# Softmax denominators from a column of ones beside the values, and a separate tile for the last sum of squares

## The chip, the cores and the metric

The kernel runs on one core of one Trainium2 chip. The metric is the device time of one execution in microseconds (us), on the slowest core where there are several; here there is one. Of several runs the median is given.

## The reference

One layer of a decoder: a half-step SwiGLU feed-forward part, a mixer, and a second half-step feed-forward part, each between two RMS norms, on 512 rows of 1024 columns in float32. The mixer runs two branches side by side and joins them with one output matrix: a gated linear recurrence (LRU) over 512 channels, and attention with a sliding window, 8 query heads of 64 columns that share 2 key and value heads, and a learned sink for each head. Cut to what the change touches:

```python
def sliding_window_sink_attention(q, k, v, sinks):      # blocks of 128 queries
    ...
    scores = jnp.einsum("bnqkgd,bnjkd->bnkgqj", qb, k_band).astype(jnp.float32) * scale
    ...
    scores = jnp.where(mask[None, :, None, None], scores, MASK_VALUE)   # window of 128 keys
    sink = sinks.astype(jnp.float32).reshape(1, 1, N_KV_HEADS, GQA_GROUP, 1, 1)
    m = jnp.maximum(jnp.max(scores, axis=-1, keepdims=True), sink)
    p = jnp.exp(scores - m)
    denom = jnp.sum(p, axis=-1, keepdims=True) + jnp.exp(sink - m)
    p = (p / denom).astype(v.dtype)
    out = jnp.einsum("bnkgqj,bnjkd->bnqkgd", p, v_band)
    ...
def reference(x, ...):
    x = x + 0.5 * rms_norm(swiglu(rms_norm(x, ffn1_pre_g), ffn1_w_gu, ffn1_w_down), ffn1_post_g)
    y = hybrid_mixer(rms_norm(x, mix_pre_g), ...)        # LRU and attention, then w_o
    x = x + rms_norm(y, mix_post_g)
    x = x + 0.5 * rms_norm(swiglu(rms_norm(x, ffn2_pre_g), ffn2_w_gu, ffn2_w_down), ffn2_post_g)
    return x
```

## The kernel before

Names: `P` is 128 (partitions, and rows of a block), `T` 512 rows, `NB` 4 blocks of rows, `HD` 64, `D` 1024, `KC` 4 chunks of 128 channels of the LRU. The instructions of each engine run in the order in which the program issues them (the schedule is written out by hand), and an engine that waits holds up all that stands behind in its queue. TensorE (PE) multiplies into the 8 banks of PSUM, which `bank(name)` hands out in turn; large products are made in three passes from a high and a low part of each operand. VectorE is `dve` (DVE), ScalarE `act` (ACT), GpSimd `pool` (POOL), the DMA queue of SyncE `sync`.

**Where the operands of the softmax live.** One wide tile `home` of 2048 columns holds four regions of 512: `k0` (first block's keys), `q0` (first block's queries), `neg` (a mask value for the first block), and `v`, the value rows turned to (key, head and column) by PE at L1512 and copied there. After the first block's scores `k0`, `q0` and `neg` are not read again.

**The softmax.** Its units are pairs (b, n): block b of 128 queries, n one of the two key heads, four query heads in each. A loop over `now` from 0 to 9 runs three stages of different units in a pipeline, and fills PE's queue in between:

- `scores(now)`: PE's products for a block when n is 0 (L1610 in the first block, L1621 after); DVE brings the part of the window that lies in the block before into one tile of 128 x 256 for two heads by a predicated copy (L1637), takes the maximum (L1638), makes the negated row maximum `nm` (L1641) and the sink's exponent `es` (L1643).
- `pump`: the next of PE's other products, those of the LRU's gates `gt`, which DVE scales (L1426).
- `turn_p(now - 1)`: PE transposes the four probability tiles (L1664), ACT copies them out (`pa`, L1666), and GpSimd masks them into the part of the block before, `pp` (L1670), and of the block itself, `pa` (L1671).
- `exps(now)`: ACT's four exponentials (L1652), each with `accum_out`, so that each is followed by a read of ACT's accumulator into `dsum`; the exponential of `es` (L1653); and GpSimd's sum of both (L1656), the denominators of the unit.
- the LRU's steps that are due: ACT's tanh and exponential, GpSimd's square `m` (L1578), DVE's `th` (L1581). At `now` 5, after the values of that step, ACT takes four square roots (L1584); at `now` 6, after the values of that step, which are those of unit (2,0), the products `xc<-xc,th` follow (L1587; two on GpSimd, two on DVE) and two scans (L1592).
- `values(now - 2)`: PE's value products into `po` (L1683, L1684); one bank holds both units of a block. After the second unit DVE takes the reciprocal of eight denominators (L1688) and multiplies 512 columns of `po` by them into `yn` (L1691); ACT squares `yn` for the norm (L1693).

After the loop come the scan of chunk 0 and the low part `wlo` of an output weight (L185, a deferred step of DVE), the root and reciprocal of the norm, the scaling of the four `yn` (L1708 on ACT, L1710 on DVE), their transposes on PE (L1762), and the output matrix.

**The tail.** The last feed-forward part ends with four blocks of rows; the last block is cut into three pieces. For each piece DVE adds the product to the sum `y` (L1983), ACT squares it with a sum into a column of the tile `ss` (L1984), and DVE multiplies it by the gain row (L1988). Then the sums are added (L1986, L1990), ACT takes the root (L1995), DVE the reciprocal (L1996), scales and adds the residual (L1999), and DMAs write the rows (L2000).

Of the kernel before, what the change touches and what calls it, by code (L numbers as in the profile page):

```python
# [8 lines left out]
F32 = mybir.dt.float32  # L9
F32R = mybir.dt.float32r  # L10
U8 = mybir.dt.uint8
AF = mybir.ActivationFunctionType
ALU = mybir.AluOpType
# [108 lines left out]
def tile_layer(ctx: ExitStack, tc: tile.TileContext, out: bass.AP, **ins: bass.AP):  # L122
# [18 lines left out]
    def bank(name):  # L141
        return psum.tile([P, T], F32, tag="bank", name=name)

    def t2k(name, dt=F32):
        return big.tile([P, T], dt, tag="t2k", name=name, bufs=NT2K)
# [16 lines left out]
    def wt(name, w=T, dt=F32):  # L162
        return tmp.tile([P, w], dt, tag="w", name=name, bufs=NW)
# [1155 lines left out]
    def masks():  # L1319

        home.append(wide("home"))
        neg = home[0][:, 2 * T:3 * T]
        upf = wt("upf")
        pool.memset(neg, 1.0)
        pool.affine_select(v4(upf), v4(neg), pattern=[[0, NB], [1, P]], base=0, channel_multiplier=-1, compare_op=ALU.is_gt, fill=0.0)
        pool.memset(neg, MASK_VALUE)
        dve.tensor_copy(up8f, upf)
        return neg
# [149 lines left out]
    mx.spread()  # L1478
    R = mx.R
    xps = [conv_in(ci, b) for ci, b in enumerate(xl_banks)]  # L1480
    k0, q0 = home[0][:, :P], home[0][:, T:2 * T]

    def in_parts(b, first, name, low=dve):

# [18 lines left out]
    for j in range(4):  # L1503
        b = in_product(f"pq{j}")
        if j < KC - 1:
            split_xc(j + 1)
        lru_gates(j)
        qT.append(in_parts(b, q0[:, j * P:(j + 1) * P], f"qT{j}", deferred if j == 3 else dve))
        if j == 0:
            vt = bank("vt")  # L1510
            for b in range(NB):
                pe.transpose(vt[:, b * P:(b + 1) * P], vT[:, b * P:(b + 1) * P], ident)  # L1512
            v = home[0][:, 3 * T:]
            dve.tensor_copy(v, vt)
    preload(AF.Exp)


# [105 lines left out]
    def scores(b, n):  # L1623
        if n == 0:
            products(b)
        mx_ = small.tile([P, 4], F32, tag="mx", name=f"mx{b}{n}")
        if b == 0:
            cur, = score_banks[b, n]
            dve.copy_predicated(cur, up8f, neg)
            dve.tensor_reduce(mx_, v4(cur), op=ALU.max, axis=AX.X)  # L1630
            heads = [cur[:, j * P:(j + 1) * P] for j in range(4)]
        else:
            heads = []
            for i, both in enumerate(score_banks[b, n]):
                both = both.rearrange("p (j w k) -> p j w k", j=2, w=2)
                cur = both[:, :, 1, :]
                dve.copy_predicated(cur, up8[:, :2, :], both[:, :, 0, :])  # L1637
                dve.tensor_reduce(mx_[:, 2 * i:2 * i + 2], cur, op=ALU.max, axis=AX.X)  # L1638
                heads += [both[:, j, 1, :] for j in range(2)]
        nm = small.tile([P, 4], F32, tag="nm", name=f"nm{b}{n}")  # L1640
        dve.scalar_tensor_tensor(nm, mx_, -scale, nsink[:, 4 * n:4 * n + 4], op0=ALU.mult, op1=ALU.min)  # L1641
        es = small.tile([P, 4], F32, tag="es", name=f"es{b}{n}")
        dve.tensor_add(es, nm, sinks[:, 4 * n:4 * n + 4])  # L1643
        unit[b, n] = heads, nm, es

    def exps(b, n):
        heads, nm, es = unit[b, n]
        dsum = small.tile([P, 4], F32, tag="dsum", name=f"dsum{b}{n}")
        sc = wt(f"sc{b}{n}")
        for j in range(4):  # L1650
            hs = slice(j * P, (j + 1) * P)
            act.activation(sc[:, hs], heads[j], AF.Exp, bias=nm[:, j:j + 1], scale=scale, accum_out=dsum[:, j:j + 1])  # L1652
        act.activation(es, es, AF.Exp)  # L1653
        if n == 0:
            unit[b] = small.tile([P, 8], F32, tag="den", name=f"den{b}")
        pool.tensor_add(unit[b][:, 4 * n:4 * n + 4], dsum, es)  # L1656
        unit[b, n] = sc

    def turn_p(b, n):
# [13 lines left out]

    def values(b, n):
        pc, pp = unit[b, n]
        if n == 0:
            unit[b, "o"] = bank(f"po{b}")
        po = unit[b, "o"]
        for j in range(4):
            hs = slice(j * P, (j + 1) * P)  # L1680
            o = po[:, (4 * n + j) * HD:(4 * n + j + 1) * HD]
            if b > 0:
                pe.matmul(o, pp[:, hs], v[:, (b - 1) * P + n * HD:(b - 1) * P + (n + 1) * HD], start=True, stop=False)  # L1683
            pe.matmul(o, pc[:, hs], v[:, b * P + n * HD:b * P + (n + 1) * HD], start=b == 0, stop=True)  # L1684
        if n == 0:
            return
        rden = small.tile([P, 8], F32, tag="rden", name=f"rden{b}")
        dve.reciprocal(rden, unit[b])  # L1688
        yn = t2k(f"yn{b}")
        h8 = lambda t: t.rearrange("p (h d) -> p h d", h=8)  # L1690
        dve.tensor_mul(h8(yn), h8(po), rden.unsqueeze(2).to_broadcast([P, 8, HD]))  # L1691
        yns.append(yn)
        sum_of = lambda: act.activation(wt(f"junk{b}"), yn, AF.Square, accum_out=ssq[:, b:b + 1])  # L1693
        if b < NB - 1:
            later(now, sum_of)
        else:
            sum_of()
# [277 lines left out]
    for tb in range(NB):  # L1975
        end = tb == NB - 1
        last = []
        ss = small.tile([P, 3], F32, tag="ss3", name=f"ss_b{tb}")
        tot = small.tile([P, 1], F32, tag="tot", name=f"tot_b{tb}")
        for i, (dh, c0, c1) in enumerate(pieces[tb]):  # L1980
            out_products(tb, i, range(f0 + 2 * ((tb, i) in started), f1))
            y = parts[tb, dh][:, c0:c1]
            dve.scalar_tensor_tensor(y, place(tb, i), -1.0 if dh else 1.0, y, op0=ALU.mult, op1=ALU.subtract if dh else ALU.add)  # L1983
            act.activation(wt(f"ysq{tb}{i}")[:, :c1 - c0], y, AF.Square, accum_out=ss[:, i:i + 1])  # L1984
            if end and i == 2:
                dve.tensor_add(tot, ss[:, 0:1], ss[:, 1:2])  # L1986
            last.append(wt(f"last{tb}{i}")[:, :c1 - c0])
            (dve if end or i else pool).tensor_mul(last[i], y, grow[dh][:, c0:c1])  # L1988
        if end:
            dve.tensor_add(tot, tot, ss[:, 2:3])  # L1990
        else:
            dve.tensor_add(tot, ss[:, 0:1], ss[:, 1:2])

        rs = small.tile([P, 1], F32, tag="rs1", name=f"rs_b{tb}")
        act.activation(rs, tot, AF.Sqrt, bias=eps4, scale=4.0 / D)  # L1995
        dve.reciprocal(rs, rs)  # L1996
        for i, (dh, c0, c1) in enumerate(pieces[tb]):
            y = parts[tb, dh][:, c0:c1]
            dve.scalar_tensor_tensor(y, last[i], rs, x_rows[tb][:, dh * T + c0:dh * T + c1], op0=ALU.mult, op1=ALU.add)  # L1999
            (act if end and i == 1 else sync).dma_start(out[0, tb * P:(tb + 1) * P, dh * T + c0:dh * T + c1], y)  # L2000
# [28 lines left out]
```

## Time and profile before

| | |
|---|---|
| time, median of 3 runs | 845.67 us (845.57 to 845.91) |
| span of the profiled execution | 843.6 us, 2.1 us below the median of the runs |
| PE busy | 834.5 us, 99% of the span |
| DVE, ACT, POOL busy | 87%, 62%, 24% |
| chain that ended last | PE 97% |
| the softmax, 405 to 462 us of the span | PE busy 56.63 of 57.00 us, DVE 51.88, ACT 47.97, POOL 33.58 |
| after the last product, 836 to 844 us | PE busy 0.67 of 8.00 us, DVE 3.62, ACT 1.60 |

The profiled execution is one run, and times within it are counted from its start. A row of a timeline gives the start and the duration in us, the engine (PEld is PE's load of weights, which overlaps its products), the line, the operation, output tile <- input tiles, the shape, and how many instructions were joined in the row; in brackets stands the idle time of the engine just before and the instruction that ended it. The durations of neighbouring instructions of PE overlap, since its passes are pipelined: the distance between their starts is what each costs. "po L1684" names tile and line.

### The profile page before, as it was taken

The numbers are of one execution on the slowest core, as the hardware profiler recorded it, in microseconds if no ns is written. First come the engines' busy times: TensorE is split into PE (matmuls) and PEld (weight loads), VectorE is DVE, ScalarE is ACT, GpSimd is POOL, SyncE is SP. The second block draws the span as 40 slices with busy tenths as digits, with TensorE's granted clock in tenths as the row PEclk, the third lists the DMA queues.
The fourth block names the chain that finished last, engine by engine and source line by source line (L and its number), as shares of the span: only waits on it lengthen the run. The fifth ranks groups of instructions, "written<-read, shape, count | busy, mean of one in ns | idle before, by whom it ended". The sixth has DMA issues, their size and how long they took to land.

```text
span 843.6 us, 12618 instructions
## 1 busy us (share of the span) xinstructions
PE 834.5 (99%) x4568; PEld 722.6 (86%) x4568; DVE 732.7 (87%) x1020; ACT 523.8 (62%) x874; POOL 201.7 (24%) x214
## 2 busy tenths in 40 slices
PE   9999999999999999999999999999999999999996
PEld 8988888988988998997788899888888888888885
DVE  4978999998979865889899589799998998998996
ACT  6646856666666655456788457436757767666552
POOL 2023000140320333334646055112004113032001
PEclk9999999999999999999999999999999999999999
DMA  7249419397595799222511131169539939769742
GB/s 251 77 131 348 151 59 322 80 254 254 129 248 185 169 261 343 77 79 91 158 50 51 50 110 42 50 137 273 186 108 231 322 91 249 249 154 262 295 137 101
DMA packets 123615, 143.75 MB, mean 170 GB/s; under 512 B 23896, under 2 KB 81568, under 8 KB 123040
## 3 DMA queue, kind: packets, MB, share of 16 engines
q1 hardware_dynamic: 109232, 111.86, 41.6%
q0 software_dynamic: 14176, 30.94, 17.0%
q8 instruction: 36, 0.59, 0.3%
q14 instruction: 27, 0.22, 0.1%
q10 hardware_dynamic: 144, 0.13, 0.0%
HBM read 100.45 MB, written 40.89 MB: 168 GB/s over the span
## 4 chain that ended last, share of the span: by engine, by line
PE 97%; ACT 1%; DVE 1%; DMA 1%; issue 0%; POOL 0%; DVEq 0%; POOLq 0%; ACTq 0%
PE ab L955 10%; PE aa L955 10%; PE da L955 5%; PE db L955 5%; PE yaa L1345 3%; PE bb L955 3%; PE ba L955 3%; PE yda L1345 2%; PE ya L507 2%; PE ya L505 2%; PE ya L506 2%; PE a_first L1205 1%; PE aa L885 1%; PE yab L1875 1%; PE yab L1874 1%; PE yab L1876 1%
## 5 line engine op out<-in xcount | busy, mean ns | idle before, releaser
L1115 POOL DMA_DIRECT2D yp_a<-stage x42 | 36.9, 1085 | 181.2 <-ACT stage L1112 160.9
L1115 POOL DMA_DIRECT2D yp_b<-stage x42 | 36.4, 1091 | 144.6 <-ACT stage L1112 121.1
L505 PE MATMUL ya<-hha,whi_ad 128*128 128x512 f32 x62 | 24.1, 389 | 0.0
L506 PE MATMUL ya<-hla,whi_ad 128*128 128x512 f32 x62 | 24.1, 389 | 0.0
L507 PE MATMUL ya<-hha,wlo_ad 128*128 128x512 f32 x62 | 24.1, 389 | 0.0
L688 POOL TENSOR_TENSOR acca_r<-acca_r,sq_r 128x512 f32<-128x512 f32 x6 | 8.2, 1359 | 51.4 <-ACT sq_r L536 51.4
L1988 POOL TENSOR_TENSOR last<-yp,grow 128x512 f32<-128x512 f32 x3 | 3.9, 1290 | 57.7 <-DVE yp L1983 57.7
L524 PE MATMUL an<-xh_mx,whi_xl 128*128 128x256 f32 x64 | 15.8, 287 | 0.0
L1984 ACT ACTIVATE ysq<-yp 128x512 f32<-128x512 f32 (+1 forms) x9 | 5.3, 585 | 16.5 <-DVE yp L1983 16.0
L525 PE MATMUL an<-xh_mx,wlo_xl 128*128 128x256 f32 x64 | 15.5, 283 | 0.0
L505 PE MATMUL gt<-xh_mx,whi_gt 128*128 128x512 f32 x32 | 14.2, 444 | 0.0
L1112 ACT COPY stage<-yab 128x512 f32<-128x512 f32 x12 | 6.5, 604 | 11.7 <-DMA yp_b<-stage 7.4
L507 PEld LDWEIGHTS ya<-hha,wlo_ad 128*128 128x128 f32 x62 | 11.6, 188 | 2.4
L506 PEld LDWEIGHTS ya<-hla,whi_ad 128*128 128x128 f32 x62 | 11.6, 188 | 2.4
L505 PEld LDWEIGHTS ya<-hha,whi_ad 128*128 128x128 f32 x62 | 11.6, 188 | 2.4
L536 ACT ACTIVATE sq_r<-yp_a 128x256 f32<-128x256 f32 (+1 forms) x10 | 5.0, 502 | 12.9 <-DVE yp_a L678 5.9
L505 PE MATMUL pq<-xh_mx,whi_q 128*128 128x512 f32 x32 | 12.8, 400 | 0.0
L505 PE MATMUL pub<-xh_f,whi_bu 128*128 128x512 f32 x32 | 12.6, 395 | 0.0
L507 PE MATMUL gt<-xh_mx,wlo_gt 128*128 128x512 f32 x32 | 12.6, 394 | 0.0
L505 PE MATMUL pgb<-xh_f,whi_bg 128*128 128x512 f32 x32 | 12.6, 393 | 0.0
L506 PE MATMUL gt<-xl_mx,whi_gt 128*128 128x512 f32 x32 | 12.5, 392 | 0.0
L580 ACT ACTIVATE xh_f<-xT,cols 128x256 fp32r<-128x256 f32 x16 | 8.1, 509 | 7.0 <-DVE xT L719 6.4
(2014 smaller groups left out, 3535.0 us busy)
## 6 DMA issues: line engine op xcount, KB each, us to landing
yp_a<-stage POOLq DMA_DIRECT2D x50, 256.0 KB, 8.9
yp_b<-stage POOLq DMA_DIRECT2D x50, 256.0 KB, 9.2
h_a<-za SPq DMA_DIRECT2D x16, 256.0 KB
hxa<-h_a SPq DMA_DIRECT2D x16, 256.0 KB
h_b<-zb SPq DMA_DIRECT2D x16, 256.0 KB
hxb<-h_b SPq DMA_DIRECT2D x16, 256.0 KB
xn<-in_x SPq DMA_DIRECT2D x8, 256.0 KB
xT_hbm<-xT POOLq DMA_DIRECT2D x2, 1024.0 KB, 9.7
```

The lines of the kernel that those rows point to most:

```text
L505: pe.matmul(ps, hi[:, k, :], xh, start=start, stop=False)
L506: pe.matmul(ps, hi[:, k, :], xl, start=False, stop=False)
L507: pe.matmul(ps, lo[:, k, :], xh, start=False, stop=stop)
L524: pe.matmul(ps[:, sl], hi[:, k, :], xh, start=k == 0, stop=False)
L525: pe.matmul(ps[:, sl], lo[:, k, :], xh, start=False, stop=False)
L885: pe.matmul(o, w[:, k, js], x, start=first and i + j + k == 0, stop=k == 3 and i == 2, skip_group_check=True)
L955: pe.matmul(b[tb], x[:, blk], w[:, k, :], start=first and q + k + j == 0, stop=q + k == 2 and j == 2, skip_group_check=True)
L1115: pool.dma_start(o, st.rearrange("p (a b) -> p a b", a=2) if len(o.shape) == 3 else st, accum_op=ALU.add)
L1205: pe.matmul(banks[j][:, HALF[0]], ws[j][part][:, k, :], n1.xs[k][xpart][:, HALF[0]], start=k == 0 and part == xpart, stop=stop and k == KD ...
L1345: pe.matmul(o, a[:, k, ms], x[:, js], start=first and i + k + m % 2 == 0, stop=k == 1 and i == 2, skip_group_check=True)
L1874: pe.matmul(banks[i], hh[:, js], hi[:, k, :], start=first and k == 0, stop=False, skip_group_check=True)
L1875: pe.matmul(banks[i], hh[:, js], lo[:, k, :], start=False, stop=False, skip_group_check=True)
```

## The change

The wide tile is divided anew: 128 columns of keys, 512 of queries, 512 of the mask value, and then 8 value groups (4 blocks by 2 key heads) of 65 columns, 64 of values and one of ones, which GpSimd sets ahead of the softmax. The value products of a head are 65 columns wide, and the 65th is the sum of the masked probabilities. So the exponentials have no `accum_out`, and `dsum` and GpSimd's sum of the denominators go. `nm` and `es` of a block are tiles of eight columns, and `es` is made once for a block, after its second unit's maximum. Each unit has a bank `po` of its own, 4 x 65 columns, and right after its value products DVE adds `es` to the four sums in PSUM, takes the reciprocal, and multiplies the unit's 256 columns into its half of `yn`. The `yn` of blocks 0 and 1 lie in `home`, where the queries and the mask value were; those of blocks 2 and 3 are tiles as before.

In the tail the last piece's sum of squares goes to a tile `ss_last` of its own. DVE makes the root's bias `tot` from the other two in two steps, and ACT's root takes `ss_last` with that bias. The gain row's multiplications of pieces 1 and 2 stand after the root, ahead of the reciprocal.

On each engine the order of all other instructions stays; GpSimd has one instruction more ahead of the softmax (the ones).

```diff
--- before.py
+++ after.py
@@ -1319,7 +1319,8 @@
     def masks():
 
         home.append(wide("home"))
-        neg = home[0][:, 2 * T:3 * T]
+        neg = home[0][:, P + T:P + 2 * T]
+        pool.memset(home[0][:, P + 2 * T:P + 2 * T + 8 * (HD + 1)].rearrange("p (h d) -> p h d", d=HD + 1)[:, :, HD:], 1.0)
         upf = wt("upf")
         pool.memset(neg, 1.0)
         pool.affine_select(v4(upf), v4(neg), pattern=[[0, NB], [1, P]], base=0, channel_multiplier=-1, compare_op=ALU.is_gt, fill=0.0)
@@ -1478,7 +1479,7 @@
     mx.spread()
     R = mx.R
     xps = [conv_in(ci, b) for ci, b in enumerate(xl_banks)]
-    k0, q0 = home[0][:, :P], home[0][:, T:2 * T]
+    k0, q0 = home[0][:, :P], home[0][:, P:P + T]
 
     def in_parts(b, first, name, low=dve):
 
@@ -1510,8 +1511,8 @@
             vt = bank("vt")
             for b in range(NB):
                 pe.transpose(vt[:, b * P:(b + 1) * P], vT[:, b * P:(b + 1) * P], ident)
-            v = home[0][:, 3 * T:]
-            dve.tensor_copy(v, vt)
+            v = home[0][:, P + 2 * T:P + 2 * T + 8 * (HD + 1)]
+            dve.tensor_copy(v.rearrange("p (h d) -> p h d", d=HD + 1)[:, :, :HD], vt.rearrange("p (h d) -> p h d", d=HD))
     preload(AF.Exp)
 
 
@@ -1637,23 +1638,24 @@
                 dve.copy_predicated(cur, up8[:, :2, :], both[:, :, 0, :])
                 dve.tensor_reduce(mx_[:, 2 * i:2 * i + 2], cur, op=ALU.max, axis=AX.X)
                 heads += [both[:, j, 1, :] for j in range(2)]
-        nm = small.tile([P, 4], F32, tag="nm", name=f"nm{b}{n}")
-        dve.scalar_tensor_tensor(nm, mx_, -scale, nsink[:, 4 * n:4 * n + 4], op0=ALU.mult, op1=ALU.min)
-        es = small.tile([P, 4], F32, tag="es", name=f"es{b}{n}")
-        dve.tensor_add(es, nm, sinks[:, 4 * n:4 * n + 4])
-        unit[b, n] = heads, nm, es
+        own = slice(4 * n, 4 * n + 4)
+        if n == 0:
+            unit[b, "nm"] = small.tile([P, 8], F32, tag="nm", name=f"nm{b}")
+        nm = unit[b, "nm"]
+        dve.scalar_tensor_tensor(nm[:, own], mx_, -scale, nsink[:, own], op0=ALU.mult, op1=ALU.min)
+        if n:
+            unit[b, "es"] = small.tile([P, 8], F32, tag="es", name=f"es{b}")
+            dve.tensor_add(unit[b, "es"], nm, sinks)
+        unit[b, n] = heads, nm[:, own]
 
     def exps(b, n):
-        heads, nm, es = unit[b, n]
-        dsum = small.tile([P, 4], F32, tag="dsum", name=f"dsum{b}{n}")
+        heads, nm = unit[b, n]
         sc = wt(f"sc{b}{n}")
         for j in range(4):
             hs = slice(j * P, (j + 1) * P)
-            act.activation(sc[:, hs], heads[j], AF.Exp, bias=nm[:, j:j + 1], scale=scale, accum_out=dsum[:, j:j + 1])
-        act.activation(es, es, AF.Exp)
-        if n == 0:
-            unit[b] = small.tile([P, 8], F32, tag="den", name=f"den{b}")
-        pool.tensor_add(unit[b][:, 4 * n:4 * n + 4], dsum, es)
+            act.activation(sc[:, hs], heads[j], AF.Exp, bias=nm[:, j:j + 1], scale=scale)
+        if n:
+            act.activation(unit[b, "es"], unit[b, "es"], AF.Exp)
         unit[b, n] = sc
 
     def turn_p(b, n):
@@ -1673,22 +1675,27 @@
 
     def values(b, n):
         pc, pp = unit[b, n]
-        if n == 0:
-            unit[b, "o"] = bank(f"po{b}")
-        po = unit[b, "o"]
+        po = bank(f"po{b}{n}")[:, :4 * (HD + 1)]
+        heads = po.rearrange("p (h d) -> p h d", h=4)
+
+        def rows(b):
+            return v[:, (2 * b + n) * (HD + 1):(2 * b + n + 1) * (HD + 1)]
+
         for j in range(4):
             hs = slice(j * P, (j + 1) * P)
-            o = po[:, (4 * n + j) * HD:(4 * n + j + 1) * HD]
+            o = po[:, j * (HD + 1):(j + 1) * (HD + 1)]
             if b > 0:
-                pe.matmul(o, pp[:, hs], v[:, (b - 1) * P + n * HD:(b - 1) * P + (n + 1) * HD], start=True, stop=False)
-            pe.matmul(o, pc[:, hs], v[:, b * P + n * HD:b * P + (n + 1) * HD], start=b == 0, stop=True)
+                pe.matmul(o, pp[:, hs], rows(b - 1), start=True, stop=False)
+            pe.matmul(o, pc[:, hs], rows(b), start=b == 0, stop=True)
+        rden = small.tile([P, 4], F32, tag="rden", name=f"rden{b}{n}")
+        dve.tensor_add(rden.unsqueeze(2), heads[:, :, HD:], unit[b, "es"][:, 4 * n:4 * n + 4].unsqueeze(2))
+        dve.reciprocal(rden, rden)
+        if n == 0:
+            unit[b, "yn"] = home[0][:, P + b * T:P + (b + 1) * T] if b < 2 else t2k(f"yn{b}")
+        yn = unit[b, "yn"]
+        dve.tensor_mul(yn[:, HALF[n]].rearrange("p (h d) -> p h d", h=4), heads[:, :, :HD], rden.unsqueeze(2).to_broadcast([P, 4, HD]))
         if n == 0:
             return
-        rden = small.tile([P, 8], F32, tag="rden", name=f"rden{b}")
-        dve.reciprocal(rden, unit[b])
-        yn = t2k(f"yn{b}")
-        h8 = lambda t: t.rearrange("p (h d) -> p h d", h=8)
-        dve.tensor_mul(h8(yn), h8(po), rden.unsqueeze(2).to_broadcast([P, 8, HD]))
         yns.append(yn)
         sum_of = lambda: act.activation(wt(f"junk{b}"), yn, AF.Square, accum_out=ssq[:, b:b + 1])
         if b < NB - 1:
@@ -1981,18 +1988,24 @@
             out_products(tb, i, range(f0 + 2 * ((tb, i) in started), f1))
             y = parts[tb, dh][:, c0:c1]
             dve.scalar_tensor_tensor(y, place(tb, i), -1.0 if dh else 1.0, y, op0=ALU.mult, op1=ALU.subtract if dh else ALU.add)
-            act.activation(wt(f"ysq{tb}{i}")[:, :c1 - c0], y, AF.Square, accum_out=ss[:, i:i + 1])
-            if end and i == 2:
-                dve.tensor_add(tot, ss[:, 0:1], ss[:, 1:2])
+            if i == 2:
+                ss_last = small.tile([P, 1], F32, tag="tot", name="ss_last")
+                act.activation(wt(f"ysq{tb}{i}")[:, :c1 - c0], y, AF.Square, accum_out=ss_last)
+                dve.tensor_scalar(tot, ss[:, 0:1], 4.0 / D, 4 * EPS, op0=ALU.mult, op1=ALU.add)
+                dve.scalar_tensor_tensor(tot, ss[:, 1:2], 4.0 / D, tot, op0=ALU.mult, op1=ALU.add)
+            else:
+                act.activation(wt(f"ysq{tb}{i}")[:, :c1 - c0], y, AF.Square, accum_out=ss[:, i:i + 1])
             last.append(wt(f"last{tb}{i}")[:, :c1 - c0])
-            (dve if end or i else pool).tensor_mul(last[i], y, grow[dh][:, c0:c1])
+            if not end or i == 0:
+                (dve if end or i else pool).tensor_mul(last[i], y, grow[dh][:, c0:c1])
+        rs = small.tile([P, 1], F32, tag="rs1", name=f"rs_b{tb}")
         if end:
-            dve.tensor_add(tot, tot, ss[:, 2:3])
+            act.activation(rs, ss_last, AF.Sqrt, bias=tot, scale=4.0 / D)
+            for i, (dh, c0, c1) in list(enumerate(pieces[tb]))[1:]:
+                dve.tensor_mul(last[i], parts[tb, dh][:, c0:c1], grow[dh][:, c0:c1])
         else:
             dve.tensor_add(tot, ss[:, 0:1], ss[:, 1:2])
-
-        rs = small.tile([P, 1], F32, tag="rs1", name=f"rs_b{tb}")
-        act.activation(rs, tot, AF.Sqrt, bias=eps4, scale=4.0 / D)
+            act.activation(rs, tot, AF.Sqrt, bias=eps4, scale=4.0 / D)
         dve.reciprocal(rs, rs)
         for i, (dh, c0, c1) in enumerate(pieces[tb]):
             y = parts[tb, dh][:, c0:c1]
```

## The prediction

> **What bounds the kernel.** I read the page first (busy time, chain that ended last), then the waits of TensorE and its weight loads, then the timelines of the engines from 405 to 462 us, where the softmax runs, and from 828 us to the end.
>
> ```profile
> span 843.6 us, 12618 instructions
> PE 834.5 (99%) x4568; PEld 722.6 (86%) x4568; DVE 732.7 (87%) x1020; ACT 523.8 (62%) x874; POOL 201.7 (24%) x214
> PE 97%; ACT 1%; DVE 1%; DMA 1%; issue 0%; POOL 0%; DVEq 0%; POOLq 0%; ACTq 0%
> PEld pt L1664 <- ACT sc L1652: 1.9, 7, 0.7
> ```
>
> TensorE (PE) is busy for 99% of the span and is 97% of the chain. So work taken from ScalarE (ACT), VectorE (DVE) or GpSimd (POOL) gains only where PE waits for it, and a delay costs as soon as PE waits. In the softmax PE waits for the exponentials, whose transposes are L1664:
>
> ```profile
> 409.33 1.05 PE L1610 MATMUL cur<-home 64*128 64x128 f32 x16
> 437.66 0.60 PE L1664 MATMUL pt<-ident,sc 128*128 128x128 f32 x4
> 440.07 0.39 PE L1683 MATMUL po<-home,pp 128*128 128x64 f32 x2
> 440.29 0.39 PE L1684 MATMUL po<-home,pa 128*128 128x64 f32 x2
> 442.41 1.38 PE L1664 MATMUL pt<-ident,sc 128*128 128x128 f32 x4 [0.28 <-ACT sc L1652]
> 446.80 1.03 PE L1664 MATMUL pt<-ident,sc 128*128 128x128 f32 x4
> 449.90 0.39 PE L1684 MATMUL po<-home,pa 128*128 128x64 f32 x2
> 456.12 1.91 PE L1762 MATMUL atp<-ident,yn 128*128 128x128 f32 x16
> ```
>
> Four transposes take 0.60 us undisturbed (437.66). Those of unit (3,0) lose 0.78 + 0.28 = 1.06 us, those of unit (3,1) 0.43 us. These two rows are the prize.
>
> **ScalarE.** The change takes out 32 reads of the accumulator.
>
> ```profile
> 434.38 0.37 ACT L1652 ACTIVATE sc<-sc,nm 128x128 f32<-128x128 f32 x1 [1.59 <-PE po L1683]
> 434.64 0.19 ACT L1652 ACTIVATION_READ_ACCUMULATOR sc<-sc,nm 128x1 f32 x1
> 434.73 0.36 ACT L1652 ACTIVATE sc<-sc,nm 128x128 f32<-128x128 f32 x1
> 454.56 1.33 ACT L1708 ACTIVATE yn<-yn,rat 128x512 f32<-128x512 f32 x2
> ```
>
> One head costs 434.73 - 434.38 = 0.35 us now, and at most 0.26 (up to the read) afterwards; I take 0.22, so that a unit of four is about 0.5 us shorter, and its last result stands 3 x 0.22 + 0.36 = 1.0 us after its start. By itself this ends the waits at 442.41.
>
> **VectorE.** Per block the change removes one reciprocal, one multiplication of 512 columns and one of two sums `es`; it adds, after each of the two value products, a sum from PSUM, a reciprocal and a multiplication of 256 columns. These wait for PE, and they stand in DVE's queue ahead of what follows.
>
> ```profile
> 420.54 1.11 DVE L1581 SCALAR_TENSOR_TENSOR th<-m,th 128x512 f32<-128x512 f32 x1
> 424.40 0.68 DVE L1581 SCALAR_TENSOR_TENSOR th<-m,th 128x512 f32<-128x512 f32 x1
> 437.35 0.16 DVE L1641 SCALAR_TENSOR_TENSOR nm<-mx,nsink 128x4 f32<-128x4 f32 x1
> 438.29 0.69 DVE L1426 TENSOR_TENSOR gt<-gt,R_mx 128x512 f32<-128x512 f32 x1
> 439.51 1.29 DVE L1587 TENSOR_TENSOR xc<-xc,th 128x512 f32<-128x512 f32 x2 [0.53 <-ACT th L1584]
> 440.73 2.33 DVE L1592 TENSOR_TENSOR_SCAN xc<-r,xc 128x512 f32<-128x512 f32 x2
> 442.97 0.41 DVE L1637 COPY_PREDICATED sc<-up,sc 128x256 f32<-128x256 uint8 x1
> 444.67 0.94 DVE L1641 SCALAR_TENSOR_TENSOR nm<-mx,nsink 128x4 f32<-128x4 f32 x1
> 448.18 0.69 DVE L1691 TENSOR_TENSOR yn<-po,rden 128x512 f32<-128x512 f32 x1
> 449.39 1.60 DVE L1592 TENSOR_TENSOR_SCAN xc<-r,xc 128x512 f32<-128x512 f32 x1
> 450.91 1.19 DVE L185 TENSOR_TENSOR wlo_wo<-raw_wo__4324,whi_wo 128x1024 fp32r<-128x1024 f32 x1
> 452.81 0.69 DVE L1691 TENSOR_TENSOR yn<-po,rden 128x512 f32<-128x512 f32 x1 [0.59 <-PE po L1684]
> ```
>
> A sum and a reciprocal of four columns I take at 0.2 each (0.16 and a step of 0.04), half a multiplication of 0.69 at 0.35: 0.75 us for a triple, bounds 0.7 and 0.9. A block then has 1.5 us in place of about 1.1. In the first four units this hides in DVE's own waits. It does not for unit (2,0). Its values end on PE at 440.29 + 0.39 = 440.68. Today DVE has finished `gt` by 438.98 and starts the multiplications and scans of `xc` at 439.51. Afterwards the new sum stands between: DVE idles until 440.7, does the triple, and starts `xc` at 441.45, **1.94 us late**. Behind it in the queue: two multiplications, two scans, then the scores of unit (3,1), for which ACT and PE wait.
>
> **What the late start meets.** From 439.51 to 442.97 DVE had GpSimd idle beside it nearly throughout (3.46 us of work). Afterwards GpSimd's masks and products fall on it:
>
> ```profile
> 419.90 1.21 POOL L1671 TENSOR_SCALAR_AFFINE_SELECT pa<-pa 128x512 f32<-128x512 f32 x1 [0.37 <-ACT pa L1666]
> 442.06 1.43 POOL L1670 TENSOR_SCALAR_AFFINE_SELECT pp<-pa 128x512 f32<-128x512 f32 x1 [5.81 <-ACT pa L1666]
> 444.31 2.52 POOL L1587 TENSOR_TENSOR xc<-xc,th 128x512 f32<-128x512 f32 x2
> 449.28 0.64 POOL L1671 TENSOR_SCALAR_AFFINE_SELECT pa<-pa 128x512 f32<-128x512 f32 x1
> ```
>
> Rows show how the two get on. `th` takes 0.68 alone and 1.11 at 420.54: the mask of 419.90 ends at 421.11, and `th` ends 0.54 later. The scan at 449.39 takes 1.60 and not 2.33 / 2 = 1.17: the mask of 449.28 ends at 449.92, the scan 1.07 later. So an instruction on SBUF waits until the other engine's ends, and they take turns (the mask at 419.90, 1.21 and not 0.64, had itself waited). The predicated copy of 442.97, which works on PSUM, ran beside the mask of 442.06 in its usual 0.41. ACT's saving starts the masks 0.5 us earlier, at about 441.5, just when DVE starts. In turns, DVE's four SBUF instructions meet two masks (0.5 each) and one or two products (1.1 each): 2.1 us more where DVE comes first, 3.2 where GpSimd does. Lower bound nothing, if they never meet; I take 2.5, between the two orders, because in both rows above the wait was complete.
>
> The Trainium skill, page "SBUF — State Buffer", section "Who interferes with whom", says that a VectorE instruction with two SBUF inputs and a GpSimd instruction that reads SBUF exclude each other, and that the order of issue decides who waits. By that rule the price is 2.1 or 3.2 us here and never nothing, and the first rival below falls away.
>
> Scores of (3,1): from the copy at 442.97 to the end of `nm`, 444.67 + 0.16, is 1.86 us (the row's 0.94 is a wait for the product of 444.31, which is over by then). Afterwards `nm` ends at 441.45 + 3.46 + 2.5 + 1.86 = 449.3, the fourth exponential 1.0 later at 450.3, and its transpose 0.3 later at 450.6; today the four end at 446.80 + 1.03 = 447.83. **PE loses 2.8 us at this place**, and the 1.06 that it gained at 442.41 goes into the wait. Bounds: 0.3 where nothing is met, 3.5 where GpSimd comes first.
>
> **Block 3.** The triple of (3,0) must now wait for PE's values (450.29 before, with the 2.8) ahead of the scan of 449.39 and the weight part of 450.91, which ran before the end of PE's last values and no longer do: 0.75 + 1.15 + 1.1 + 0.75 = 3.75 after 450.29 is 454.0 for the last `yn`, against 452.81 + 0.69 = 453.5: 0.5 late beyond PE's own delay. From there over ACT's square and scaling (ends 454.56 + 1.33 = 455.89) to PE's second transpose at 456.12 + 0.11 there is slack of 0.3. **PE loses another 0.2 us**, bounds 0 and 0.7. From here to 836 us PE waits almost nowhere, so all of it reaches the tail.
>
> **The tail.**
>
> ```profile
> 836.39 0.28 PE L1852 MATMUL ybl<-whi_br,hlb 128*128 128x256 f32 x1
> 836.56 0.42 DVE L1988 TENSOR_TENSOR last<-yp,grow 128x256 f32<-128x256 f32 x1
> 836.91 0.42 DVE L1983 SCALAR_TENSOR_TENSOR yp<-ybl,yp 128x256 f32<-128x256 f32 x1
> 836.95 0.19 ACT L1984 ACTIVATION_READ_ACCUMULATOR ysq<-yp 128x1 f32 x1
> 837.70 0.42 ACT L1984 ACTIVATE ysq<-yp 128x256 f32<-128x256 f32 x1 [0.56 <-DVE tot_b L1986]
> 838.02 0.19 ACT L1984 ACTIVATION_READ_ACCUMULATOR ysq<-yp 128x1 f32 x1
> 838.43 0.29 ACT L1995 ACTIVATE rs_b<-tot_b,eps 128x1 f32<-128x1 f32 x1 [0.23 <-DVE tot_b L1990]
> 838.76 0.16 DVE L1996 RECIPROCAL rs_b<-rs_b 128x1 f32<-128x1 f32 x1 [0.36 <-ACT rs_b L1995]
> ```
>
> PE's last product ends at 836.67; the gain row's multiplication at 836.56 no longer stands before the last sum, which starts at 836.71 and not 836.91. ACT's last square waited 0.56 us for DVE's read of the tile `ss`; with a tile of its own it starts at 837.17, its result is read out by 837.68, and the root follows at 837.72 on the same engine, not at 838.43. Its bias (two one-column steps, done by 837.5) is ready. The two multiplications that now stand before the reciprocal end their turn at 838.1, the root at 838.05: reciprocal at 838.1 in place of 838.76. **Gain 0.7 us**, bounds 0.4 and 0.75.
>
> **At nothing.** 65 columns in place of 64: a pass of 64 columns costs 440.29 - 440.07 = 0.22 for two, a pass of 128 (two row groups side by side, 16 in 1.05) about 0.12; so columns are not what sets 0.11. Lower bound nothing (no pass is dropped), upper 1/64 of 112 passes x 0.11 = 0.2. The column of ones is set on GpSimd ahead of the softmax, where nobody waits for it. The second PSUM bank of a block makes later products wait for triples of earlier units, which are done before their turn. The eight sums that leave GpSimd cost nobody anything today.
>
> **The sum.** +2.8 + 0.2 - 0.7 = +2.3 us on the span of 843.6; the runs' median, 845.67, holds 2.1 us around the span, which the change does not touch: **848.0 us**.
>
> **Rivals.** (1) No turns between DVE and GpSimd, only the late start: +0.3 + 0.4 - 0.7 = 0: 845.7 us. For it: no row has these very instructions together. Against: both rows with SBUF on either side show full waits. It decides if GpSimd's masks and products run before 441.4 or after 444.9. Chance 0.25. (2) Faster: DVE's scores of (3,1) come in time, PE keeps 1.06 + 0.43 = 1.5 at the exponentials, with the tail -2.2: 843.5 us. It is one mechanism, ACT's 32 reads gone at the two rows where PE waits for ACT, and it holds if `nm` of (3,1) ends by 445.1, when PE would come for it; that is 4.2 us before my value and 1.7 before that without turns; 0.07. (3) The odd row of 65 columns slows a pass by 0.02 us: 112 x 0.02 = 2.2 more, 850.2 us; no row speaks for it; 0.06.
>
> **Numbers.** The forecast has 0.62. Its own range is 847.3 to 849.3; with rival 1 the range is 845.4 to 849.6, which leaves out rivals 2 and 3 and some edges. A difference of 0.2% (1.7 us) is about what can be told from no change. Slower by more: nearly all of the forecast's case and rival 3, 0.65; faster 0.07; within 0.28.
>
> **What would show it.** After: DVE idle for some 1.7 us before a sum `rden<-po`, released by PE, near 440.7; `xc` products and scans of both engines overlapping up to 447.5 with doubled times; transposes of (3,1) waiting for ACT for over 2 us; no such wait at the unit before; the last reciprocal 1.4 us after PE's last product ends, not 2.1. If the scans keep 1.17 us each, the turns were wrong; if `po` passes exceed 0.11 us, rival 3.

## The result, and the profile after

| | us |
|---|---|
| before, median of 6 runs | 845.71 (844.72 to 846.19) |
| after, median of 6 runs | 850.44 (848.24 to 853.36) |
| ratio | 1.0058, 95% interval 1.0043 to 1.0072 |
| profiled execution of after | time 848.77, span 847.1 (before 843.6) |
| forecast | 848.0, range 845.4 to 849.6 |

The change is slower, as forecast, but by twice as much: 4.7 us and not 2.3, and so above the forecast's range. Its six runs fall into two groups: 848.24, 848.77 and 849.43 at a mean granted clock of 0.997 (the share of its full clock that PE got over the run), and 851.46, 852.79 and 853.36 at 0.990 to 0.992; the runs of the kernel before show 0.997 to 0.999. The profiled execution is one of the first group. The page of after (busy line, chain) and the waits of PE and of its weight loads; lines have moved down, L1664 is now L1666, L1652 is L1656, L1587 is L1588 and L1592 is L1593:

```profile
span 847.1 us, 12591 instructions
PE 835.5 (99%) x4568; PEld 723.0 (85%) x4568; DVE 734.2 (87%) x1032; ACT 520.9 (61%) x838; POOL 200.2 (24%) x207
PE 90%; DVE 6%; ACT 2%; issue 2%; DMA 1%; DVEq 0%; POOL 0%; ACTq 0%; POOLq 0%
PE pt L1666 <- ACT sc L1656: 2.9, 1, 2.9
PEld pt L1666 <- ACT sc L1656: 3.6, 2, 3.4
```

The busy shares say nothing, and the chain's 6% of DVE (some 50 us, before 1%) misleads: about 35 us of it lie between 540 and 601 us, where the chain was followed back from a wait of PE of only 0.49 us. What the change made is the piece from 440.92 to 448.66, which runs over DVE and ACT to the one wait of 2.9 us. The timelines of DVE and GpSimd show what stands behind it:

```profile
437.74 0.69 DVE L1427 TENSOR_TENSOR gt<-gt,R_mx 128x512 f32<-128x512 f32 x1
440.17 0.16 DVE L1691 TENSOR_TENSOR rden<-po,es 128x4 f32<-128x4 f32 x1 [1.74 <-PE po L1689]
440.92 1.72 DVE L1588 TENSOR_TENSOR xc<-xc,th 128x512 f32<-128x512 f32 x2
442.56 3.80 DVE L1593 TENSOR_TENSOR_SCAN xc<-r,xc 128x512 f32<-128x512 f32 x2
446.29 0.40 DVE L1638 COPY_PREDICATED sc<-up,sc 128x256 f32<-128x256 uint8 x1
447.98 0.16 DVE L1645 SCALAR_TENSOR_TENSOR nm<-mx,nsink 128x4 f32<-128x4 f32 x1
441.13 0.97 POOL L1672 TENSOR_SCALAR_AFFINE_SELECT pp<-pa 128x512 f32<-128x512 f32 x1 [7.46 <-ACT pa L1668]
442.17 0.97 POOL L1673 TENSOR_SCALAR_AFFINE_SELECT pa<-pa 128x512 f32<-128x512 f32 x1
443.11 4.32 POOL L1588 TENSOR_TENSOR xc<-xc,th 128x512 f32<-128x512 f32 x2
```

DVE idles 1.74 us for PE's values of (2,0), does the triple, and starts `xc` at 440.92. Multiplications and scans take 5.52 us (before 1.29 + 2.33 = 3.62), GpSimd's two products 4.32 (before 2.52): the turns. PE's timeline at the same place (the first two rows are of the kernel before), and the engines' busy time in four stretches of after (columns: PE, PEld, DVE, ACT, POOL busy, then PE's granted clock, DMA share, GB/s):

```profile
447.91 0.39 PE L506 MATMUL gt<-xl_mx,whi_gt 128*128 128x512 f32 x1
448.14 0.39 PE L507 MATMUL gt<-xh_mx,wlo_gt 128*128 128x512 f32 x1
441.41 1.08 PE L1666 MATMUL pt<-ident,sc 128*128 128x128 f32 x4
445.32 0.40 PE L507 MATMUL gt<-xh_mx,wlo_gt 128*128 128x512 f32 x1
448.66 1.25 PE L1666 MATMUL pt<-ident,sc 128*128 128x128 f32 x4 [2.94 <-ACT sc L1656]
450.13 0.63 PE L506 MATMUL gt<-xl_mx,whi_gt 128*128 128x512 f32 x1
450.56 0.63 PE L507 MATMUL gt<-xh_mx,wlo_gt 128*128 128x512 f32 x1
453.04 0.39 PE L1689 MATMUL po<-home,pa 128*128 128x65 f32 x2
459.80 0.33 PE L1769 MATMUL atp<-ident,home 128*128 128x128 f32 x1 [0.28 <-ACT home L1715]
840.64 0.28 PE L1859 MATMUL ybl<-whi_br,hlb 128*128 128x256 f32 x1
```

```profile
441.40:445.70 4.30, 4.30 (x27) 3.35 (x26) 4.30 (x4) 3.26 (x8) 4.23 (x4) 1.00 0.02 4
445.70:448.70 3.00, 0.06 (x2) 0.05 (x1) 2.86 (x8) 0.47 (x2) 2.93 (x3) 1.00 0.00 0
448.70:452.12 3.42, 3.42 (x13) 2.89 (x14) 1.91 (x6) 2.41 (x7) 1.29 (x3) 0.50 0.00 0
452.12:460.00 7.88, 7.60 (x49) 6.52 (x49) 5.76 (x13) 4.64 (x10) 3.62 (x2) 1.00 0.27 86
```

Here is what the prediction has no word for: after the wait PE runs for 3.4 us at half its clock. Two passes that start 0.23 us apart before (447.91 to 448.14) start 0.43 apart (450.13 to 450.56), and the 3.4 us cost about 1.3 (1.86 to 3.14 in the table). PE's starts in both profiles, matched one to one:

| place | before | after | after - before |
|---|---|---|---|
| transposes of (3,0) | 442.41 | 441.41 | -1.00 |
| transposes of (3,1) | 446.80 | 448.66 | +1.86 |
| last values of (3,0) | 449.90 | 453.04 | +3.14 |
| second transpose `atp` | 456.23 | 459.80 | +3.57 |
| last product | 836.39 | 840.64 | +4.25 |
| end of the span | 843.63 | 847.07 | +3.43 |

Of the first row 0.32 is older than the softmax: PE is that much earlier from the first 23 us on, where the profiles of the experiments lie between 0.7 earlier and 0.3 later.

### The profile page after: what moved, and what is told of

The parts are those of the page before. It is cut to its first block, busy times and chain, and to the rows that moved or that the text cites. A ratio compares the mean times of both kernels' runs of the same rounds, so it can differ in the third digit from the quotient of the medians.

```text
span 847.1 us, 12591 instructions
## 1 busy us (share of the span) xinstructions
PE 835.5 (99%) x4568; PEld 723.0 (85%) x4568; DVE 734.2 (87%) x1032; ACT 520.9 (61%) x838; POOL 200.2 (24%) x207
## 4 chain that ended last, share of the span: by engine, by line
PE 90%; DVE 6%; ACT 2%; issue 2%; DMA 1%; DVEq 0%; POOL 0%; ACTq 0%; POOLq 0%
PE aa L955 10%; PE ab L955 10%; PE da L955 5%; PE db L955 4%; PE yaa L1346 3%; PE bb L955 3%; PE ba L955 3%; PE yda L1346 2%; PE ya L507 2%; PE ya L506 2%; PE ya L505 2%; PE a_first L1205 1%; PE aa L885 1%; PE yab L1882 1%; PE yab L1881 1%
## 5 line engine op out<-in xcount | busy, mean ns | idle before, releaser
L506 PE MATMUL pq<-xl_mx,whi_q 128*128 128x512 f32 x32 | 12.5, 390 | 0.0
```

The source lines that it names most:

```text
L506: pe.matmul(ps, hi[:, k, :], xl, start=False, stop=False)
```

## The experiments

### Where the loss is made

**The tail alone**, on the kernel before: its hunk of the diff and nothing else.

> The kernel before with the change of the tail alone. Theory (the tail gains 0.8 us after PE's last product, and the softmax loses the rest): PE's last product as before, the time from its end to the end of the span 6.15 us and not 6.96, so 0.8 us faster: 844.9 against 845.7. Rival (the tail's change also costs something ahead of the end, in PE's last 300 us): no gain, 845.7 or more.

844.42 us, ratio 0.9988 (0.9980 to 0.9997). From PE's last start (835.89) to the end of the span (842.40) it is 6.51 us, before 7.24: 0.73 gained there. Of the 1.23 us by which this profile's span is shorter, the other 0.5 is older than the tail: PE is 0.74 us earlier from the first 20 us on and loses 0.3 of it again near 596 us. Whether the medians, 1.3 us apart, hold the same half microsecond is not shown.

**The softmax alone**: the change with the tail of before.

> The change without its tail. Theory: all of the loss is made in the softmax and the clock that follows its wait, so 0.8 us slower than the whole change: about 851 us at the median (849 where the clock comes back after one window of 3.4 us, up to 854 where it takes longer), 3 to 8 us above the kernel before. Rival (part of the loss is the tail's): no slower than the whole change, 850.4 or less.

852.28 us, ratio 1.0072 (1.0056 to 1.0088); runs 848.9 to 853.6. The profiled execution, 852.24, was one of the long ones, and its stretches show why:

```profile
445.60:447.26 1.66, 0.02 (x1) 0.00 (x0) 1.62 (x4) 0.00 (x0) 1.66 (x1) 1.00 0.00 0
447.26:448.50 1.24, 0.00 (x0) 0.00 (x0) 1.14 (x4) 0.37 (x2) 1.17 (x3) 0.50 0.00 0
448.50:460.92 12.42, 12.37 (x47) 11.18 (x48) 6.34 (x16) 5.71 (x15) 4.76 (x5) 0.50 0.17 53
460.92:470.00 9.08, 9.08 (x49) 7.71 (x49) 7.85 (x13) 7.43 (x14) 2.92 (x2) 1.00 0.12 43
```

The same wait, 2.9 us, but the clock falls 1.7 us into it and stays halved for 13.65 us, although PE is busy for all of the last 12.4. PE is 1.75 us late at the transposes of (3,1) and 7.25 late afterwards: 5.5 us lost to the clock alone. From there to the last product it stays at 7.28, so the half microsecond that after loses more near 596 us, at a wait of PE for a ScalarE tile (0.49 us), is not the change's; the tail alone loses 0.3 us there.

**The triple of (2,0) behind the scans**, in DVE's queue:

```diff
-        dve.tensor_add(rden..., heads[:, :, HD:], es...); dve.reciprocal(rden, rden); dve.tensor_mul(yn..., rden...)
+        held.append(norm) if (b, n) == (2, 0) else norm()      # norm: the same three
...
             for ci in (2, 3):
                 scan(ci)
+            while held: held.pop()()
```

> The change, with the sum, reciprocal and multiplication of unit (2,0) behind the two scans in DVE's queue, and nothing else moved. Theory (the loss comes from this one wait ahead of the products and scans of xc): DVE starts the products at about 438.5 us as before, scans take about 1.2 each, nm of (3,1) is ready near 446, PE waits there about 1 us instead of 2.9, the granted clock stays at full in the softmax, and the runs lie together within 1 us: 845 us. Rival A (DVE has too much work in these units, wherever it stands): PE still waits over 2.5 us at the transposes of (3,1), 848 to 853. Rival B (the banks or the 65 columns cost it): 848 or more with no such wait.

844.67 us, ratio 0.9991 (0.9982 to 0.9999), runs 844.0 to 845.3. DVE's and PE's rows:

```profile
438.64 1.29 DVE L1588 TENSOR_TENSOR xc<-xc,th 128x512 f32<-128x512 f32 x2 [0.16 <-ACT th L1585]
439.85 2.33 DVE L1593 TENSOR_TENSOR_SCAN xc<-r,xc 128x512 f32<-128x512 f32 x2
446.33 1.10 PE L1667 MATMUL pt<-ident,sc 128*128 128x128 f32 x4 [0.43 <-ACT sc L1657]
```

Three instructions of 0.75 us together, moved past four others on one engine, are worth 5.8 us against the change. Products and scans have their old durations. That shows where the loss begins; neither DVE's work nor banks nor the 65th column cost it.

### The clock behind the wait

**PE kept busy in its wait**: transposes of the identity into the bank that the real ones then overwrite, first 24, then 12.

```diff
         pt = bank(f"pt{b}{n}")
+        for j in range(24 if (b, n) == (NB - 1, 1) else 0):      # 12 in the second run
+            pe.transpose(pt[:, :P], ident, ident)
```

> The change, with 24 transposes of the identity ahead of the transposes of unit (3,1), into the bank that these then overwrite: about 2.1 us of work for PE inside its wait of 2.9 us. Theory (the wait costs 3 us itself, and a halved clock behind it costs 1.3 us or more and makes the runs differ): DVE, ACT and the wait's end as in the change, no stretch of half clock after it, passes of the value products 0.22 us for two and not 0.42, runs within 1 us of each other: about 847 us. Rival (the half clock has another cause than the idle PE, and comes anyway): 850.4 with runs 5 us apart.

> The change, with 12 transposes of the identity ahead of the transposes of unit (3,1) and not 24: the wait's end as in the change, PE idle in it for about 1.6 us and not 2.9 or 0.3. If the clock is halved only by waits longer than that: as with 24, 847 to 847.6 us. If 1.6 us do it as well: runs at 848 to 849.5 and at 851 to 853.5, as in the change.

```profile
445.23 2.78 PE L1665 MATMUL pt<-ident 128*128 128x128 f32 x24
448.32 1.10 PE L1668 MATMUL pt<-ident,sc 128*128 128x128 f32 x4 [0.31 <-ACT sc L1656]
446.10 1.47 PE L1665 MATMUL pt<-ident 128*128 128x128 f32 x12
449.20 1.10 PE L1668 MATMUL pt<-ident,sc 128*128 128x128 f32 x4 [1.63 <-ACT sc L1656]
```

With 24 (first two rows) the real transposes still start late, and DVE's scans still take 3.80, but no stretch is halved: 847.41 us, ratio 1.0028 (1.0017 to 1.0039), every run at a clock of 0.998 or more. Useless work on PE makes the changed kernel 3 us faster. The runs do not lie within 1 us, as expected: two of the seven, 848.94 and 849.07, are 1.4 us above the rest at a full clock, for a cause that no profile shows. With 12 the idle time is 1.63 us, and the ten runs fall in two: five at 846.7 to 847.8 with a clock of 0.998 or 0.999, five at 852.5 to 853.5 with 0.991. Both expectations came true, each in half of the runs. So 1.6 us can be enough, and whether it is changes from run to run. The profile is of a run with the full clock; that the others waited as long is taken from the kernel being the same.

### The turns of DVE and GpSimd

**GpSimd's products later**, behind its masks of (3,0), and then one step later still, behind those of (3,1); the wait ahead of `xc` stays.

```diff
-            for ci in range(KC):                  # now == 6
+            for ci in (2, 3):
                 root_u(ci)
...
             turn_p(*units[now - 1])
+        if now == 7:                              # 8 in the second run
+            for ci in (0, 1):
+                root_u(ci)
```

> The change, with GpSimd's two products of xc behind its masks of unit (3,0) instead of ahead of them, so that DVE's two scans have GpSimd idle beside them; the wait ahead of xc stays. Theory (turns on SBUF: the four instructions took 5.5 us where they took 3.6 before): the scans take about 2.3 us for both and not 3.8, nm of (3,1) is ready 1.5 to 1.9 us earlier, PE waits about 1.2 us and not 2.9, the clock stays at full: 845 to 845.5 us. Rival (the scans are slow for another reason, such as the late start alone): scans still 3.8 us, PE waits 2.9, 848 to 853.

> The change, with GpSimd's two products of xc behind its masks of unit (3,1), one step later than in the run that put them behind the masks of (3,0); the wait ahead of xc stays. Theory of turns: no product of GpSimd is left beside the scans, nm and es, so the scans take 2.3 to 2.5 us for both, nm of (3,1) is done 1.2 us earlier than in the change, and PE's wait is 1.7 us and not 2.9. If so short a wait leaves the clock at full: 846 to 846.7 us with all runs within 1.5 us; if it halves the clock too: 848 to 851. Rival (no turns): wait 2.9, 848 to 853.

850.9 us (1.0058, 1.0042 to 1.0074) and 850.7 (1.0068, 1.0056 to 1.0080). Three rows of the first, then four of the second:

```profile
442.38 2.76 DVE L1593 TENSOR_TENSOR_SCAN xc<-r,xc 128x512 f32<-128x512 f32 x2
446.76 0.77 DVE L1645 SCALAR_TENSOR_TENSOR nm<-mx,nsink 128x4 f32<-128x4 f32 x1
448.04 1.10 PE L1666 MATMUL pt<-ident,sc 128*128 128x128 f32 x4 [2.50 <-ACT sc L1656]
440.69 1.72 DVE L1588 TENSOR_TENSOR xc<-xc,th 128x512 f32<-128x512 f32 x2
442.33 2.76 DVE L1593 TENSOR_TENSOR_SCAN xc<-r,xc 128x512 f32<-128x512 f32 x2
446.71 0.16 DVE L1645 SCALAR_TENSOR_TENSOR nm<-mx,nsink 128x4 f32<-128x4 f32 x1
447.38 1.10 PE L1666 MATMUL pt<-ident,sc 128*128 128x128 f32 x4 [1.91 <-ACT sc L1656]
```

Without the products the scans take 2.76 and not 3.80. In the first run `nm` then waits 0.6 us for the product that used to meet the scans, and PE's wait is 2.50; in the second it does not, and the wait is 1.91. So the turns move as the theory says. The first run missed its sizes all the same: the scans were expected at 2.3 us, PE's wait at 1.2 and the time at 845 to 845.5, since a mask still met the scans and the product met `nm`. The second came near its own (2.3 to 2.5, and 1.7), and its time is in the 848 to 851 that was expected if so short a wait halves the clock too. Neither run is faster than the change: the clock was halved for 10.24 us in both profiles.

### What is left of the gain

**All first units' triples late** (behind the next unit's scores; (3,0)'s behind the scan and weight part), **the same with the reads kept** (`accum_out` into a tile that nobody reads), and **with the scans of chunks 2 and 3 behind the scores of (3,1)**.

```diff
+        held.append(norm) if n == 0 else norm()          # all three; run behind scores(now), at now == 8 behind deferred.run()
+            act.activation(..., accum_out=dsum[:, j:j + 1])   # second only
+            if now == 7: scan(2); scan(3)                     # third only, ahead of the held triple; no longer at now == 6
```

> The change, with the sum, reciprocal and multiplication of every first unit of a block behind the scores of the unit that follows; for (3,0) behind the scan and the weight part of DVE. Theory: (3,1)'s scores come 0.75 us earlier than with the one triple behind the scans, PE keeps the 0.85 us that it gains at (3,0), and with the tail's 0.8 us or more: 843.9 to 844.3 us. Rival (the softmax part gives nothing even so, since the gain is lost again at block 3): 844.4 to 844.9, as the tail alone.

> As the kernel with every first unit's triple late, but the exponentials keep accum_out, whose sums nobody reads. Theory (the 32 reads that the change takes from ACT are what PE gains at (3,0), 0.85 us): 0.7 to 1.0 us slower than that kernel, about 844.9, with PE waiting at the transposes of (3,0) as before. Rival (the gain has another source, such as the sums es that go): within 0.3 us of that kernel.

> As the kernel with every first unit's triple late, and the scans of chunks 2 and 3 behind the scores of unit (3,1) as well. Theory (what PE waits for at (3,1) is DVE's queue ahead of its scores): nm of (3,1) is ready near 443.5 us, PE waits neither there nor at (3,0) beyond 0.4 us, gains 1.2 to 1.6 us in the softmax, and with the tail 2.0 to 2.4: 843.3 to 843.7 us. Rival (the scans, now beside the masks and later values, give the time back at block 3's norm): 844 or more, PE waiting at the transposes of yn.

844.38 us (0.9988, 0.9979 to 0.9996), 844.62 (0.9991, 0.9982 to 0.9999) and 849.34 (1.0048, 1.0036 to 1.0060). The first waits nowhere at (3,1) and still has the wait for the reciprocal and scaling of block 3: it equals the tail alone, so the rival holds and the softmax part gives nothing that can be measured. The second fell on its rival's side, within 0.3 us, but says little about the reads: 0.24 us is within the noise, and its held triple of (0,0) came so late that PE waited 1.1 us for the bank. The third missed. Five of its six runs, 848.25 to 850.62 at a clock of 0.992 to 0.994, lost clock as well, and no profile shows their waits. The profile is of the sixth, 845.66 at 0.999. In it PE had its transposes in time and waited for masks instead:

```profile
443.29 3.36 DVE L1593 TENSOR_TENSOR_SCAN xc<-r,xc 128x512 f32<-128x512 f32 x2
443.32 4.41 POOL L1588 TENSOR_TENSOR xc<-xc,th 128x512 f32<-128x512 f32 x2
448.83 0.44 PE L1689 MATMUL po<-home,pp 128*128 128x65 f32 x2 [1.15 <-POOL pp L1673]
```

The scans now meet both products, and the masks of (3,0) stand behind these.

**Scans and products late together**, and the same orders in the kernel before with the new tail.

```diff
+        if now == 7: root_u(0); root_u(1)      # behind turn_p, in addition to the late scans
```

> Every first unit's triple late, the scans of chunks 2 and 3 behind the scores of unit (3,1), and GpSimd's two products behind its masks of (3,0), so that scans and products no longer meet ahead of these masks. Theory (with the scans late, PE waited 1.2 us for a mask that stood behind the products): no PE wait for masks nor at the transposes of (3,1); PE gains 1.2 to 1.6 us in the softmax; with the tail 843.2 to 843.8 us. Rival (any such order loses as much at block 3 as it wins at (3,1)): 844.2 to 844.7, as with the triples late alone.

> The kernel before with the new tail, and the scans and products of the run above late in the same way; no column of ones, sums by accum_out as before. Theory (the column of ones is worth what the reads take at (3,0), about 0.4 us, and no more): 0.3 to 0.6 us slower than the run above. Rival (the column is worth nothing, its triples eat it): the same as that run within 0.2 us.

847.95 us (1.0035, 1.0022 to 1.0048) and 849.76 (1.0047, 1.0035 to 1.0059). Neither comes near its expectation. In the first the scans are back at 2.33, but the masks of (3,1) stand behind the products and take turns with DVE's scan of chunk 0 and its weight part:

```profile
442.94 2.33 DVE L1593 TENSOR_TENSOR_SCAN xc<-r,xc 128x512 f32<-128x512 f32 x2
451.15 1.50 POOL L1674 TENSOR_SCALAR_AFFINE_SELECT pa<-pa 128x512 f32<-128x512 f32 x1
451.13 0.43 PE L1689 MATMUL po<-home,pp 128*128 128x65 f32 x2 [1.34 <-POOL pp L1673]
452.70 0.44 PE L1690 MATMUL po<-home,pa 128*128 128x65 f32 x2 [1.13 <-POOL pa L1674]
```

Waits of 1.34 and 1.13 us, and a halved stretch of 3.41 us; 6.83 us in the other. With a different wait in each, the two do not compare the column of ones.

## Where the prediction was right, and where it failed

- **DVE's late start**: forecast 1.94 us. DVE was 0.55 early (gt 438.29 to 437.74), so `xc` starts 440.92 - (439.51 - 0.55) = 1.96 late. The triple, forecast 0.75, took 440.17 to 440.92.
- **The turns**: forecast 2.5, between the 2.1 and 3.2 of the two orders; measured 5.52 - 3.62 = 1.90, of which GpSimd's product 3.80 - 2.76 = 1.04 and two masks 0.43 each. Right in kind, 0.6 too dear: DVE came first, and only one product came in between, so that the lower of the two orders, 2.1, was the one that came. The Trainium skill, page "SBUF — State Buffer", section "Who interferes with whom", is borne out in that each of the three meetings took time.
- **ScalarE**: four exponentials take 1.14 us, so a step is (1.14 - 0.37) / 3 = 0.26, the forecast's upper bound, and not the 0.22 that it took. Its saving did not end the waits at (3,0): the four transposes take 1.08, 0.48 more than undisturbed; 0.6 of 1.06 came back.
- **PE's loss at (3,1)**: forecast 2.8 at the end of its transposes; 449.91 - 447.83 + 0.32 = 2.4. With PE kept busy in its wait they end at 448.32 + 1.10 = 449.42 in a profile that is 0.63 early, so 2.2; the other 0.2 is already the clock.
- **Block 3**: forecast 0.2, bounds 0 and 0.7; 3.57 - 3.14 = 0.43. (The first rival puts 0.4 here and the sum 0.2; the prediction gives no working for the 0.4.)
- **The tail**: forecast 0.7; 7.24 - 6.43 = 0.81, by the steps that it named and a little over its upper bound of 0.75.

```profile
840.96 0.42 DVE L1990 SCALAR_TENSOR_TENSOR yp<-ybl,yp 128x256 f32<-128x256 f32 x1 [0.18 <-PE ybl L1859]
841.41 0.42 ACT L1993 ACTIVATE ysq<-yp 128x256 f32<-128x256 f32 x1
841.96 0.29 ACT L2003 ACTIVATE rs_b<-ss_last,tot_b 128x1 f32<-128x1 f32 x1
842.29 0.16 DVE L2009 RECIPROCAL rs_b<-rs_b 128x1 f32<-128x1 f32 x1
```

The reciprocal starts 842.29 - 840.92 = 1.4 us after the last product's end, as forecast.

- **65 columns**: two passes still start 0.22 us apart. The third rival is dead; so is the first, by the turns, and the second, by the wait of 2.9 us.

**The step that failed** is "PE loses 2.8 us at this place": the sum took the wait for its whole price. It carries no term for what PE does after idling, and that cost 1.3 us in the profiled execution, 5.5 in the longest profile and, at the median, more than the wait itself. With PE kept busy in its wait the change costs 847.41 - 845.70 = 1.7 us, against the 2.3 of the sum, and lies inside the forecast's own range. That it comes so near is in part luck: the sum's terms measured 2.2, 0.4 and -0.8 against 2.8, 0.2 and -0.7, so that errors cancel. The rest of the 4.7, 3.0 us, is the clock. The Trainium skill, page "TensorE: Matmul & The Clock Gate", section "Part 1: The HAM clock gate (the "warmup" mystery)", names the means: a free-running window of 3.413 us and a clock halved after an idle window. By that rule, read strictly, a wait of 2.9 us would not do it; the measurements disagree and decide: a wait of 2.9 us did it in both profiles shown, the one of 1.9 in all of its five runs (clock 0.990 to 0.992), the one of 1.6 in five of ten.

The traces let one say more. The changes of clock lie on a grid of 3.413 us, and the place of the wait on it differs from run to run. The step of the grid just before the clock fell held 2.94 us without a product of PE in the profile of after, 1.65 in the softmax alone (the rest of its wait lies in the next step), 1.75 and 1.70 in the two runs with GpSimd's products later, and 1.89 and 1.93 in the last two runs. In the softmax of no profile did a step with less than 1.65 make it fall; the nearest is 1.48, with 12 transposes, where the other 0.15 us of the wait lies in the next step. So idle time within one step of the grid sorts the waits, with a border near half a step, and the length of a wait alone does not. The border is not sharp by this measure: behind the last product, in the profile with 12 transposes, a step with 1.69 us idle kept the clock, and the late scans lost the clock in five runs although their profile shows no step with more than 1.15. This was read from fourteen profiles and tried in no experiment.

Why a run gets one step of half clock or four is open. A mean clock of 0.996 or 0.997 goes with one in the profiles, 0.995 with two, 0.992 with three and 0.990 with four.

## What to carry to other kernels

Where TensorE is the bound, a wait of its own of 1.6 us or more, or two shorter ones close together (1.34 and 1.13 us), is not priced by its length: it can cost another 1.3 to 5.5 us by the clock behind it, so keep TensorE busy or make the wait shorter, and look at the spread of the runs and their granted clocks, since one profile shows only one outcome. Before an instruction that waits for TensorE is put into VectorE's queue, look at what stands behind it and has no such wait; moving three small instructions behind four others turned a loss of 4.7 us into a gain of 1.0 (the tail's). A reordering of VectorE and GpSimd moves their turns to the next instruction that somebody waits for, so follow each one to TensorE before it is believed.

## What the runs showed of the hardware

The half-clock stretches lasted 3.41, 6.83, 10.24 and 13.65 us, one to four times 3.413, and began 440.32, 443.73 or 447.15 us (129, 130 or 131 times 3.413) after the clock had first come to full. PE lost about 0.4 to 0.5 us for each microsecond of them (1.28 us in 3.41, 5.5 in 13.65, 4.8 in 10.24). The clock did not come back after the first busy window: in the longest stretch PE was busy for the last 12.4 us and still ran at half.
